# Input projection of a hybrid decoder layer: gates, keys and values 512 columns wide

## The chip, the cores and the metric

The kernel runs on one core of a Trainium2 chip. Its engines work from queues of their own, each strictly in order: TensorE (PE, matrix products into PSUM), VectorE (DVE), ScalarE (ACT), GpSimd (POOL) and SyncE (SP, which here only issues DMA transfers). They wait for each other through semaphores. The metric is the time of one execution on the device in microseconds (us); lower is better. The median of three runs of the kernel before is 3501.9 us (3501.55 to 3503.35).

## What is computed

One step of a decoder layer for one prompt of 2048 tokens and 8 sampled sequences of 8 tokens, all in float32. Cut to what matters here:

```python
z = einsum('bsd,dc->bsc', x, w_in)              # 1024 -> 3600 columns, for 2048 + 64 tokens
fq, fk, fv = z[..., 0:512], z[..., 512:1024], z[..., 1024:1536]   # attention, 8 heads of 64
flogf = log_sigmoid(z[..., 1536:1544] + b_fox_f)
qk = silu(causal_conv4(z[..., 1544:2568]))      # mLSTM queries and keys, 4 heads of 128
mv = z[..., 2568:3080]; ig, lf = gates of z[..., 3080:3088]
og = sigmoid(z[..., 3088:3600] + b_og)          # output gates
fox_h = forgetting attention (prompt: causal; samples: over 8192 cached tokens each)
m_h   = mLSTM: per head a 128 x 128 state, carried from chunk to chunk
x1 = layer_norm(a * x + concat(fox_h, norm(m_h) * og) @ w_o)
y  = layer_norm(a * x1 + square(relu(x1 @ w1)) @ w2)
```

`fk`, `fv`, the states and several small tensors are outputs too.

## The kernel before

The work runs in phases: A, the input projection (some 0 to 988 us); B, the prompt's attention; O, the output projection; C, the two matrices of the MLP. Two side streams run beside them. One is the mLSTM (`gate_stream`, `m_block`, `m_sample`), which has to end with phase A. The other is the sampled tokens' attention (`sample_attention`), which goes on to the end.

Every float32 product is made of three in the format fp32r. `split_hi` (ACT, L130) rounds an operand to its high part, `split_lo` (DVE, L133) takes the rest, and `mm3` (L138 to L140) adds hi x hi, hi x lo and lo x hi over 8 row tiles of 128. One group is thus 24 matmuls into one PSUM bank (`pm`, four banks).

Phase A goes over four blocks of tokens: the first has the 64 sampled tokens (tile 16) and four tiles of 128, the others four tiles. `load_x` transposes a tile's x on PE and splits it. Before, a block has two pairs of buffers, `xh0`/`xl0` (320 columns) and `xh1`/`xl1` (256). `wload` brings 256 (or 272) columns of `w_in` as two pieces of four row tiles: a raw slot `wra` (two of them), then a `whi` and a `wlo` slot (four of each), 4 x 272 numbers per partition. A load takes two of the four slots, and the next load can fill the other two.

A block makes, in this order: mLSTM values with the gate columns (two loads); mLSTM queries and keys, eight groups of 128 channels with a convolution behind them (four loads); output gates (two); attention queries (two); keys (two); values (two). "Natural" passes (`natural`: values, gates, keys) have tokens on the partitions: x is the stationary operand, a tile's 24 matmuls stream 256 weight columns, and a `sink` copies the bank out (`st`, four buffers of 256) and stores it. The query and key groups have channels on the partitions: weights are stationary and 320 or 256 token columns stream, two matmul groups for one block. The last tile of the values' second pass starts the next block's `load_x`.

`tick(us)` is called after each group with the time that the group is supposed to take. It emits one step of the mLSTM stream for each 2.8 us (`PACE_M`) and one step of the sampled attention for each 7.5 us. A step runs to the next `yield`. `beside` binds its instructions behind the latest ones of the main stream; beyond this, the final order in each engine's queue is set by a planner that simulates the program while it is built, and an engine then keeps that order.

The mLSTM works through 16 chunks of 128 tokens, four a block (`m_block`, L576 on). A chunk's products are the scores `pS` (L604) and transposed keys `pk` (L611) in the one `mm` bank, the numerators of two pairs of heads (L621, L622) and the state's updates (L629) in the one `mn` bank. After `norm_out` (statistics on DVE, a power and the gating on POOL) come the output transposes (L561), in the `mm` bank again, and ACT's copy of them (L563). L645 takes the last state out. In the changed kernel these lines are numbered higher by 6: L610, L617, L627, L628, L635, L567, L569, L651; the first transpose of phase B, L835, is L841.

After the last block, the steps of the mLSTM stream that are left are emitted one behind the other, and then phase B:

Of the kernel before, what the change touches and what calls it, by code (L numbers as in the profile page):

```python
# [19 lines left out]
# microseconds of the main stream's products per step of a side stream  # L20
# [24 lines left out]
C_O = 3088  # L45
# [7 lines left out]
def body(ctx, tc, I, O, stages):  # L53
# [3 lines left out]
    # ------------------------------------------------------------------ constants  # L57
# [25 lines left out]
    # pools of the sampled tokens' attention, which runs beside all phases, and of the mLSTM  # L83
# [6 lines left out]
    sqk = []                                         # new k of the sampled tokens  # L90
# [4 lines left out]
    gm = pm.tile([128, 16, 8], F32, name="gm")      # g = i - b and m, tokens on partitions  # L95
# [6 lines left out]
    def beside(gen):  # L102
        """one step of a side stream, whose instructions queue behind the main stream's latest"""
        with ExitStack() as es:
            for i in last.values():
                es.enter_context(tc.issue_after(i.ins))
            return next(gen, 0)

    def tick(us):
        """keeps the side streams in step with the main one"""  # L110
# [45 lines left out]
    # ------------------------------------------------------------------ phase A: input projection  # L156
# [16 lines left out]
    # conv weights transposed: [128 ch, 8 groups, 5] with the factor 1/2 of silu(c) = c/2 (1 + tanh(c/2))  # L173
# [38 lines left out]
    def wload(cols):  # L212
        """columns of w_in, [(first, number), ...], in their two parts, for each of the 8 row tiles"""
        n = sum(c[1] for c in cols)
        H, L = [], []
        for kg in range(2):
            wr = pa.tile([128, 4 * 272], F32, name="wra", bufs=2)[:, :4 * n].rearrange("p (k c) -> p k c", k=4)
            o = 0
            for c0, m in cols:
                SY.dma_start(wr[:, :, o:o + m], w_in[kg * 512:(kg + 1) * 512, c0:c0 + m].rearrange("(k p) c -> p k c", p=128))  # L220
                o += m
            wh = pa.tile([128, 4 * 272], F32R, name="whi", bufs=4)[:, :4 * n].rearrange("p (k c) -> p k c", k=4)
            wl = pa.tile([128, 4 * 272], F32R, name="wlo", bufs=4)[:, :4 * n].rearrange("p (k c) -> p k c", k=4)
            split_hi(wh, wr)
            split_lo(wl, wr, wh)
            H += [wh[:, k] for k in range(4)]
            L += [wl[:, k] for k in range(4)]
        return H, L
# [6 lines left out]
    xT = {}  # L235
# [10 lines left out]

    def load_x(bi, tiles):
        """the block's x with channels on partitions, in two parts; column tiles of two token tiles"""
        blk, pre, off = geom(bi)
        for t in tiles:  # L250
            i = int(off[t] >= pre + 256)
            if len(xT.setdefault(bi, [])) == i:
                w = 256 if i else 320
                xT[bi].append((pa.tile([128, 8, w], F32R, name=f"xh{i}"), pa.tile([128, 8, w], F32R, name=f"xl{i}")))
# [3 lines left out]
            (xh, xl), s = xcol(bi, t)  # L258
            for hf in range(2):
# [3 lines left out]
                dh = xh[:, hf * 4:hf * 4 + 4, s]  # L263
                split_hi(dh, px[:, :, :n])
                split_lo(xl[:, hf * 4:hf * 4 + 4, s], px[:, :, :n], dh)

    def xcol(bi, t):
        """column tile and columns of a token tile"""
        blk, pre, off = geom(bi)
        o = off[t]  # L270
        i = int(o >= pre + 256)
        o -= i * (pre + 256)
        return xT[bi][i], slice(o, o + tok_n(t))

    def gate_stream(bi):
# [4 lines left out]
        def gates(z, lg, shape, bb):  # L280
# [16 lines left out]
            # log1p(e) = ln(u) + (e - (u - 1)) / u  # L297
# [21 lines left out]
        def rowset(cols, base, n_el, np_, sample):  # L319
# [32 lines left out]
            # M = m - b (kept in lr), ar = m0 - M, g = i - b  # L352
# [28 lines left out]
            # back to tokens on partitions: g, m  # L381
# [13 lines left out]
    def block_a(bi):  # L395
# [3 lines left out]
        def natural(sink, *cols, hook=None):  # L399
            wh, wl = first.pop() if first else wload(cols)  # L400
            for i, t in enumerate(blk):
# [4 lines left out]
                (xh, xl), s = xcol(bi, t)  # L406
                for k in range(8):
                    mm3(ps, xh[:, k, s], xl[:, k, s], wh[k], wl[k], k == 0, k == 7)
                sink(t, m, ps)
                tick(2.6)  # L410

        def stage(ps, m, n):
            st = pa.tile([128, 256], F32, name="st", bufs=4)[:m, :n]
            A.copy(st, ps)
            return st
# [12 lines left out]
        # mLSTM q/k, channels on partitions, causal convolution along the free axis  # L428
        for j in range(8):
# [8 lines left out]
            for i in range(2):  # L438
                xh, xl = xT[bi][i]
                w = 256 + (pre if i == 0 else 0)  # L440
                ps = ppa.tile([128, 512], F32, name="pm", tag="pm", bufs=4)[:, :w]
                for k in range(8):
                    mm3(ps, wh[k][:, cs], wl[k][:, cs], xh[:, k, :w], xl[:, k, :w], k == 0, k == 7)
                tick(w * 0.01)
                if w == 320:
                    A.copy(qs[:, :, 3:11], ps[:, 0:64].rearrange("p (b t) -> p b t", t=8))
                A.copy(qi[:, 3 + i * 256:259 + i * 256], ps[:, w - 256:])  # L447
# [18 lines left out]
        if pre:  # L466
            # conv state of the sampled sequences
# [16 lines left out]
        for i in range(2):  # L484
            def sink(t, m, ps, i=i):
                r = tok_r(t)
                cs = slice(i * 256, (i + 1) * 256)
                st = pa.tile([128, 256], F32, name="st", bufs=4)[:m]
                V.tensor_tensor(st, ps, bog[:m, cs], op=OP.add)  # L489
                A.activation(st, st, AF.Tanh, scale=0.5)  # L490
                V.scalar_tensor_tensor(st, st, 1.0, nwh[:m, cs], op0=OP.add, op1=OP.mult)
                SY.dma_start(dog[r:r + m, cs], st)
            natural(sink, (C_O + i * 256, 256))
        gated.add(bi)
        # attention q, scaled, channels on partitions; that of the sampled tokens as [channel % 32, sequence, channel // 32, t]
        for j in range(4):
            if j % 2 == 0:
                wh, wl = wload([(j * 128, 256)])
                if pre:
                    qr = ps_.tile([32, 8, 8, 8], F32, name="qr", bufs=1)  # L500
            cs = slice((j % 2) * 128, (j % 2) * 128 + 128)
            st = pa.tile([128, 512], F32, name="qst", tag="ac", bufs=3)
            for i in range(2):
                xh, xl = xT[bi][i]
                w = 256 + (pre if i == 0 else 0)
                ps = ppa.tile([128, 512], F32, name="pm", tag="pm", bufs=4)[:, :w]
                for k in range(8):
                    mm3(ps, wh[k][:, cs], wl[k][:, cs], xh[:, k, :w], xl[:, k, :w], k == 0, k == 7)
                tick(w * 0.01)
                if w == 320:  # L510
                    for c in range(4):
                        V.tensor_scalar(qr[:, :, (j % 2) * 4 + c], ps[c * 32:c * 32 + 32, 0:64].rearrange("p (b t) -> p b t", t=8), 0.125, None, op0=OP.mult)
                A.activation(st[:, i * 256:i * 256 + 256], ps[:, w - 256:], AF.Copy, scale=0.125)
# [3 lines left out]
        for i in range(2):  # L517
            def sink(t, m, ps, i=i):
                d = k_out(t)[:, i * 256:(i + 1) * 256]
                if t == 16:  # L520
                    if i == 0:
                        sqk.append(pm.tile([64, 512], F32, name="sqk", tag="qk", bufs=1))
                    st = sqk[0][:, i * 256:(i + 1) * 256]
                    A.copy(st, ps)
                else:
                    st = stage(ps, m, 256)
                SY.dma_start(d, st)
            natural(sink, (512 + i * 256, 256))
        for i in range(2):
            def sink(t, m, ps, i=i):  # L530
                d = v_out(t)[:, i * 256:(i + 1) * 256]
                SY.dma_start(d, stage(ps, m, 256))
            natural(sink, (1024 + i * 256, 256),
# [933 lines left out]
```

## Time and profile before

| | |
|---|---|
| median of three runs | 3501.9 us |
| profiled execution: span | 3492.4 us |
| what lies around the span, against the median | 9.5 us |
| PE busy in the span | 3354.9 us, 96% |
| ACT, DVE, POOL busy | 1366.6, 2178.9, 897.4 us |
| mean granted TensorE clock | 0.985 |

The page gives no time of the profiled execution apart from its span, so the 9.5 us are against the runs' median.

How to read the rows. A page's row of groups has the line, the engine, the operation, the tile written and those read, the shapes and the count; then busy time and the mean of one in ns; then the engine's idle time just before them and what ended it. A row of the timeline has the start in us from the span's start, the length in us, the engine, the line, the operation and the count of instructions merged; in brackets the idle time ahead of it and who ended it. Matmuls are pipelined and their ends are modelled, so that neighbours overlap: what one costs in a stream is the distance of two starts. SPq is SP's queue of DMA issues. A row of windows has, for each stretch, its length, each engine's busy time and count, the TensorE clock, the DMA engines' mean busy share, and GB/s.

### The profile page before, as it was taken

Reading aid. Unit: us, or ns where it says so; the run is one execution under the profiler, and the core shown is the slowest. Engines: PE = TensorE matmul, PEld = TensorE weight load, DVE = VectorE, ACT = ScalarE, POOL = GpSimd, SP = SyncE. Lnnn points to the kernel's source line nnn. Section 1 sums busy time; section 2 is a strip of 40 time slices with the busy share of each in tenths; the row PEclk is TensorE's granted clock in tenths of the full one; section 3 lists DMA queues with packets and bytes.
Section 4 is the critical chain, followed back from the end, with each engine's and each line's share of the span. In section 5 each row is a group of like instructions: output and inputs, shape, how many; then the busy total and the mean of one; then the engine's idle time right before and its main releaser. Section 6 shows DMA issues by size and latency. Waiting matters only on the chain.

```text
span 3492.4 us, 59522 instructions
## 1 busy us (share of the span) xinstructions
PE 3354.9 (96%) x22428; PEld 2670.1 (76%) x22428; DVE 2178.9 (62%) x5302; ACT 1366.6 (39%) x2818; POOL 897.4 (26%) x942
## 2 busy tenths in 40 slices
PE   8899899999989999999899999999999999999998
PEld 8898778888866666667567677677677777898887
DVE  6747747657558787655556567666666544654555
ACT  3333323334358888512324243332233333443332
POOL 1013213231322222265332324223324111100000
PEclk9999999999999999999899999999999999999999
DMA  6557777775853232586776767768768555442221
GB/s 198 167 167 223 223 220 237 245 246 174 275 163 86 75 81 57 172 275 215 273 250 197 266 214 262 258 200 271 253 218 296 192 164 176 148 154 73 85 85 64
DMA packets 446040, 663.15 MB, mean 190 GB/s; under 512 B 84604, under 2 KB 333760, under 8 KB 444856
## 3 DMA queue, kind: packets, MB, share of 16 engines
q1 hardware_dynamic: 369064, 380.13, 36.1%
q0 software_dynamic: 74304, 270.57, 22.5%
q10 hardware_dynamic: 2384, 8.65, 0.7%
q8 instruction: 176, 2.88, 0.3%
q14 instruction: 112, 0.92, 0.1%
HBM read 598.01 MB, written 61.22 MB: 189 GB/s over the span
## 4 chain that ended last, share of the span: by engine, by line
PE 69%; DMA 15%; DVE 6%; issue 5%; POOL 3%; ACT 1%; SPq 0%; POOLq 0%; DVEq 0%; ACTq 0%
PE py L138 7%; PE py L140 6%; PE py L139 6%; PE ph L138 6%; PE ph L139 6%; PE ph L140 6%; DMA kraw<-cache_k,idxK 4%; PE po L919 4%; DMA vt<-cache_v,idxV 4%; PE pt L910 4%; PE pm L138 4%; PE pm L139 3%; PE pm L140 3%; PE sO L1406 3%; PE pS L871 2%
## 5 line engine op out<-in xcount | busy, mean ns | idle before, releaser
L1150 DVE TENSOR_TENSOR y<-y,py 128x512 f32<-128x512 f32 (+1 forms) x476 | 319.3, 680 | 251.1 <-PE py L140 246.9
L138 PE MATMUL ph<-x1h,wh 128*128 128x512 f32 (+1 forms) x1280 | 455.5, 356 | 2.4 <-ACT wh L130 2.4
L130 ACT ACTIVATE wh<-wr 128x1024 fp32r<-128x1024 f32 x264 | 273.4, 1057 | 466.0 <-PE py L140 264.0
L139 PE MATMUL ph<-x1l,wh 128*128 128x512 f32 (+1 forms) x1280 | 454.7, 355 | 0.0
L140 PE MATMUL ph<-x1h,wl 128*128 128x512 f32 (+1 forms) x1280 | 453.7, 355 | 0.2 <-DVE wl L133 0.2
L1401 POOL DMA_INDIRECT vt<-cache_v,idxV x256 | 257.9, 1007 | 736.1 <-PE sO L1406 701.2
L1316 DVE STREAM_TRANSPOSE kT<-kraw 128x512 f32<-128x512 f32 x512 | 328.3, 684 | 179.8 <-DMA kraw<-cache_k,idxK 178.4
L138 PE MATMUL py<-wh,hh 128*128 128x512 f32 (+1 forms) x1088 | 431.6, 399 | 1.5 <-DVE y L1148 0.8
L139 PE MATMUL py<-wl,hh 128*128 128x512 f32 (+1 forms) x1088 | 429.6, 395 | 0.7 <-DVE wl L133 0.7
L140 PE MATMUL py<-wh,hl 128*128 128x512 f32 (+1 forms) x1088 | 429.1, 395 | 0.0
L1314 POOL DMA_INDIRECT kraw<-cache_k,idxK x256 | 280.9, 1097 | 571.3 <-DVE kT L1316 439.0
L133 DVE TENSOR_TENSOR wl<-wr,wh 128x1024 fp32r<-128x1024 f32 x264 | 333.2, 1269 | 91.4 <-PE ph L140 25.7
L138 PE MATMUL pm<-whi,xh 128*128 128x256 f32 (+2 forms) x1088 | 320.3, 294 | 7.5 <-DVE st L489 4.8
L139 PE MATMUL pm<-wlo,xh 128*128 128x256 f32 (+2 forms) x1088 | 315.7, 290 | 0.0
L140 PE MATMUL pm<-whi,xl 128*128 128x256 f32 (+2 forms) x1088 | 315.4, 290 | 0.0
L138 PEld LDWEIGHTS ph<-x1h,wh 128*128 128x128 f32 x1280 | 240.9, 188 | 46.5 <-issue 11.1
L140 PEld LDWEIGHTS ph<-x1h,wl 128*128 128x128 f32 x1280 | 240.7, 188 | 42.8 <-issue 11.1
L139 PEld LDWEIGHTS ph<-x1l,wh 128*128 128x128 f32 x1280 | 240.6, 188 | 40.4 <-issue 8.6
L138 PEld LDWEIGHTS py<-wh,hh 128*128 128x128 f32 (+1 forms) x1088 | 201.3, 185 | 62.7 <-issue 18.1
L140 PEld LDWEIGHTS py<-wh,hl 128*128 128x128 f32 (+1 forms) x1088 | 201.3, 185 | 55.5 <-issue 9.9
L139 PEld LDWEIGHTS py<-wl,hh 128*128 128x128 f32 (+1 forms) x1088 | 201.5, 185 | 48.5 <-issue 8.6
L138 PE MATMUL pm<-xh,whi 128*128 128x256 f32 (+1 forms) x768 | 224.7, 293 | 0.8 <-ACT qi L447 0.8
(359 smaller groups left out, 6875.1 us busy)
## 6 DMA issues: line engine op xcount, KB each, us to landing
wr<-w SPq DMA_DIRECT2D x256, 512.0 KB
wra<-w_in SPq DMA_DIRECT2D x112, 512.0 KB
xn<-x_prompt SPq DMA_DIRECT2D x32, 512.0 KB
Rb<-dR SPq DMA_DIRECT2D x128, 128.0 KB
dqk<-th SPq DMA_DIRECT2D x32, 256.0 KB
qk<-dqk SPq DMA_DIRECT2D x16, 512.0 KB
qn<-dq SPq DMA_DIRECT2D x128, 64.0 KB
wr<-w_o SPq DMA_DIRECT2D x16, 512.0 KB
```

The source lines that it names most:

```text
L130: last["ACT"] = A.activation(dst, src, AF.Copy, scale=scale)
L133: r = (eng or V).tensor_tensor(dst, src, hi.bitcast(F32), op=OP.subtract)
L138: T.matmul(ps, wh, xh, start=first, stop=False)
L139: T.matmul(ps, wh, xl, start=False, stop=False)
L140: last["PE"] = T.matmul(ps, wl, xh, start=False, stop=stop)
L910: T.transpose(pt[:, k], sc[i][0][k0 // 4][:, k * 128:(k + 1) * 128], ident)
L919: last["PE"] = T.matmul(po[c:c + 64, q0:], z["vn"][:, k], PT[:, k - k0, q0:], start=(k < 2), stop=(k >= nk - 2), skip_group_check=True)
L1150: V.tensor_tensor(y, y, ps, op=OP.add)
L1314: G.indirect_dma_start(out=kraw, out_offset=None, in_=ck, in_offset=IO(ap=idxK[:, b, kt + k, f:f + 1], axis=0))
L1316: V.transpose(z["kT"][:, k, 2 * f + i].rearrange("p b c -> p (b c)"), kraw[:, i * 512:(i + 1) * 512])
L1401: G.indirect_dma_start(out=vt.rearrange("p f c -> p (f c)"), out_offset=None, in_=cv, in_offset=IO(ap=idxV[:, b, pg * 4 + u, f:f + 1], axi ...
L1406: T.matmul(po[r:r + 32], z["PT"][:, hg, 2 * f + g, pg].rearrange("p h q -> p (h q)"), vt[:, g, hg * 256:(hg + 1) * 256], start=(kt == 0 an ...
```

## The change

Output gates, attention keys and attention values are projected in one pass of 512 columns each. Their load comes as four pieces of two row tiles, into the same slots; one load fills all four. A block's x lies in one pair of buffers (`xh`, `xl`, made once), in block 0 as 320 and 256 columns for each row tile, in the later blocks tile after tile, so that a group with channels on the partitions streams 512 columns as four runs of 128. `st` has three buffers of 512, a wide natural group ticks 5.2 once, and `qr` takes the slot of `Rb`. mLSTM values with the gate columns, and the weight loads of queries and keys, stay at 256 or 272 columns.

```diff
 def wload(cols):
-        for kg in range(2):
-            wr = pa.tile([128, 4 * 272], F32, name="wra", bufs=2)[:, :4 * n]...
+        q = 4 if n <= 272 else 2
+        for kg in range(8 // q):
+            wr = pa.tile([128, 4 * 272], F32, name="wra", bufs=2)[:, :q * n]...
...
+    xh = pa.tile([128, 36 * 128], F32R, name="xh")
+    xl = pa.tile([128, 36 * 128], F32R, name="xl")
...
+    def xpiece(bi):
+        if bi == 0:
+            return [(320, *(x[:, :2560].rearrange("p (k c) -> p k c", k=8) for x in (xh, xl))),
+                    (256, *(x[:, 2560:].rearrange("p (k c) -> p k c", k=8) for x in (xh, xl)))]
+        return [(512, *(x[:, :4096].rearrange("p (t k c) -> p k t c", t=4, k=8) for x in (xh, xl)))]
...
 def natural(sink, *cols, hook=None):
-                    mm3(ps, xh[:, k, s], xl[:, k, s], wh[k], wl[k], k == 0, k == 7)
+                    mm3(ps, th[:, k], tl[:, k], wh[k], wl[k], k == 0, k == 7)
                 sink(t, m, ps)
-                tick(2.6)
+                tick(2.6 if wh[0].shape[1] < 512 else 5.2)
 def stage(ps, m, n):
-            st = pa.tile([128, 256], F32, name="st", bufs=4)[:m, :n]
+            st = pa.tile([128, 512], F32, name="st", bufs=3)[:m, :n]
...
-            for i in range(2):
-                xh, xl = xT[bi][i]
-                w = 256 + (pre if i == 0 else 0)
+            for w, th, tl in xpiece(bi):
                 ps = ppa.tile([128, 512], F32, name="pm", tag="pm", bufs=4)[:, :w]
                 for k in range(8):
-                    mm3(ps, wh[k][:, cs], wl[k][:, cs], xh[:, k, :w], xl[:, k, :w], k == 0, k == 7)
+                    mm3(ps, wh[k][:, cs], wl[k][:, cs], th[:, k], tl[:, k], k == 0, k == 7)
                 tick(w * 0.01)
...
-            natural(sink, (C_O + i * 256, 256))
+        natural(sink, (C_O, 512))
...
-                    qr = ps_.tile([32, 8, 8, 8], F32, name="qr", bufs=1)
+                    qr = ps_.tile([32, 8, 8, 8], F32, name="qr", tag="Rb", bufs=1)
...
-            natural(sink, (512 + i * 256, 256))
+        natural(sink, (512, 512))
...
-            natural(sink, (1024 + i * 256, 256),
-                    hook=None if i == 0 or bi == 3 else lambda n: load_x(bi + 1, BLKS[bi + 1][0:1]) if n == len(blk) - 1 else None)
+        natural(sink, (1024, 512),
+                hook=None if bi == 3 else lambda n: load_x(bi + 1, BLKS[bi + 1][0:1]) if n == len(blk) - 1 else None)
```

105 lines of the change are left out of this document (50 added, 55 removed).

## The prediction

> **What bounds the kernel now.** I read the page first (engines, chain), then three windows, then the end of the projection in order of time.
>
> ```profile
> span 3492.4 us, 59522 instructions
> PE 3354.9 (96%) x22428; PEld 2670.1 (76%) x22428; DVE 2178.9 (62%) x5302; ACT 1366.6 (39%) x2818; POOL 897.4 (26%) x942
> PE 69%; DMA 15%; DVE 6%; issue 5%; POOL 3%; ACT 1%; SPq 0%; POOLq 0%; DVEq 0%; ACTq 0%
> L138 PE MATMUL pm<-whi,xh 128*128 128x256 f32 (+2 forms) x1088 | 320.3, 294 | 7.5 <-DVE st L489 4.8
> ```
> ```profile
> core 0: us, PE busy (x) PEld busy (x) DVE busy (x) ACT busy (x) POOL busy (x), PEclk, DMA share, GB/s
> 0.00:988.00 988.00, 920.77 (x7692) 843.84 (x7693) 621.60 (x1725) 330.25 (x714) 236.50 (x251) 0.98 0.70 214
> 988.00:1001.40 13.40, 4.72 (x30) 3.56 (x29) 6.21 (x27) 3.34 (x9) 5.24 (x9) 0.83 0.74 196
> 1001.40:3492.40 2491.00, 2429.39 (x14711) 1822.67 (x14709) 1551.07 (x3550) 1032.97 (x2095) 655.67 (x682) 0.99 0.56 180
> ```
> PE is busy 96% of the span and carries 69% of the chain. The projection (0 to 988) keeps PE at 921 of 988 us, so a shorter stream of products shortens it. The 13.4 us behind it are another regime: PE works 4.72 us of them and waits otherwise. There the mLSTM's last chunk finishes with no products beside it, and prompt attention begins only behind it:
>
> ```profile
> 987.64 0.28 PE L140 MATMUL pm<-whi,xl 128*128 128x256 f32 x1
> 987.76 0.38 PE L621 MATMUL mn<-va,Wm 128*128 128x129 f32 x2
> 990.20 0.49 PE L621 MATMUL mn<-va,Wm 128*128 128x129 f32 x2 [1.38 <-ACT hh L573]
> 992.72 0.71 PE L629 MATMUL mn<-va,kw 128*128 128x129 f32 x4 [1.36 <-ACT hh L573]
> 999.35 1.12 PE L561 MATMUL mm<-ident,hh 128*128 128x128 f32 x4 [4.51 <-POOL hh L557]
> 1001.19 0.38 PE L645 MATMUL mm<-ident,Cs 128*4 128x128 f32 x1 [0.72 <-ACT ot L563]
> 1001.36 1.91 PE L835 MATMUL pt<-ident,dup 128*128 128x128 f32 x8
> ```
> The last product starts at 987.64, the attention's first transpose at 1001.36: an open tail of 13.7 us.
>
> **The change, part by part.** The sum is made against the profiled execution: span 3492.4, which lies 9.5 us under the 3501.9 median of the runs; I take those 9.5 as unchanged and add the difference to the median.
>
> *Wider products.* Natural groups of output gates, k and v: 17 token tiles x 3 kinds x 24 matmuls = 1224 of 512 columns in place of 2448 of 256. Channel groups: 12 x 24 x 3 blocks = 864 in place of 1728 (block 0 keeps 320 + 256). What one costs on the path is start to start, not its busy time:
>
> ```profile
> 304.88 0.28 PE L140 MATMUL pm<-xh,wlo 128*128 128x256 f32 x1
> ...
> 309.31 0.28 PE L138 MATMUL pm<-xh,whi 128*128 128x256 f32 x1
> ```
> ```profile
> 1899.63 0.39 PE L139 MATMUL ph<-x1l,wh 128*128 128x512 f32 x1
> ...
> 1900.77 0.39 PE L138 MATMUL ph<-x1h,wh 128*128 128x512 f32 x1
> ```
> 37 steps between the first two: 4.43 / 37 = 0.1197 us. 5 between the others: 1.14 / 5 = 0.228. A pair saves 0.239 - 0.228 = 0.0114 us; x 2088 = **-24 us**. In blocks 1 to 3 the streamed operand becomes four pieces of 128 columns, 4 KB apart, which no fp32r row here shows: the upper end is 0.239 for these 864 (nothing saved, -14 in all). The lower end is the rounding of the rows, 0.01 us over 5 steps: 0.226, -28. I take 0.228, as each piece is contiguous.
>
> The Trainium skill (TensorE: Matmul & The Clock Gate, section Back-to-back issue gap) puts a lone warm matmul at N / 2.4 + 2.5 ns, so a pair would save 2.5 ns, an estimate of -5 us where the rows give -24, and the total 19 us later. The trace disagrees: its 256-column pitch lies 13 ns over 256 / 2.4, not 2.5.
>
> *Weights.* Four pieces of two row tiles fill all four `whi`/`wlo` slots, so a 512-wide load cannot lie ready beside another, and only two raw pieces (`wra`, two slots) wait ahead.
>
> ```profile
> 404.01 0.38 SPq L220 DMA_DIRECT2D wra<-w_in  x1
> ...
> 944.42 0.37 SPq L220 DMA_DIRECT2D wra<-w_in  x1
> ```
> ```profile
> 408.85 1.06 ACT L130 ACTIVATE whi<-wra 128x1024 fp32r<-128x1024 f32 x1 [2.23 <-DMA wra<-w_in]
> ...
> 957.00 1.06 ACT L130 ACTIVATE whi<-wra 128x1024 fp32r<-128x1024 f32 x1
> ```
> ```profile
> L130 ACT ACTIVATE whi<-wra x112: 1039/1058/1121, 6.1 to 957.0; 128x1024 fp32r<-128x1024 f32 x104, 128x1088 fp32r<-128x1088 f32 x8
> L133 DVE TENSOR_TENSOR wlo<-wra,whi x112: 1179/1224/2351, 7.2 to 958.1; 128x1024 fp32r<-128x1024 f32 x104, 128x1088 fp32r<-128x1088 f32 x8
> ```
> From k to v, clock from the start of k's last tile (24 x 0.228 = 5.5 us): the first slot is free after 6 matmuls, 1.4; + 1.06 + 1.22 = 3.7, when the raw slot is free and the third raw piece can be issued on SP's queue; landed and waited for 4.84 later, 8.5; split 9.6. In the changed kernel's PE order, block 1 has 20 products and 4 transposes of v ahead of the first that needs that piece: 5.5 + 20 x 0.228 = 10.0. So the row with nothing else in the way just fits. The split queues behind other ACT and DVE work and the load behind others on SP: lower end 0, upper end 8 us a block (the projection's last load is split 12.6 after its issue, 944.42 to 957.00, its wait for a slot included; 12.6 - 4.84). I take 2 us x 4 for v, 1 us in all for q behind the gates: **+9**, range 0 to 31. The other passes find two slots freed a pass earlier.
>
> The Trainium skill (Trainium Kernel Development and Optimization, section Best Practices) says to double-buffer so that DMA and compute overlap; before did it, this gives it up for 512-wide loads. No row prices it at a boundary here.
>
> *One x buffer, three `st` of 512, `qr` on `Rb`'s slot.* A token tile's columns are overwritten only after its own v products, three tiles earlier than the rewrite, so nothing. Half as many evictions, twice as wide, lie beside PE (PE's idle before `pm<-whi,xh` products is 7.5 us in the page's row). The stores keep their bytes. `qr` is done before the first `Rb` load. Zero; the cover is the product stream, and without it each eviction would show with its copy:
>
> ```profile
> 984.70 0.37 ACT L414 COPY st<-pm 128x256 f32<-128x256 f32 x1 [4.15 <-PE pm L140]
> ```
>
> *Side streams.* `tick(5.2)` once for two `tick(2.6)`: as many steps, two at a time. Here the PE order of the changed kernel speaks. Numbers behind names count tiles as they are made:
>
> ```
> before 6197 L611 mm_11792 (pk, last chunk)  next to pm_11764, pm_11803
> before 6222 L140 pm_11803  = last product;  6223 L621 ... 6237 L645, 6238 L835 attention
> after  4046 L617 mm_8473   (pk, chunk 12)   inside pm_9317; made before pm_8498 (row 3662)
> after  4092 L140 pm_9381   = last product;  4093 L635, 4097 L567 (chunk 12)
> after  4100 L610, 4118 L610, 4136 L610 (chunks 13, 14, 15)  ... 4154 L651, 4155 L841 attention
> ```
> Before, the mLSTM stands level with the products at the end; after, it runs most of a block's second half behind, and **three whole chunks** queue in order between the last product and the attention, with nothing among them. Price of an uncovered chunk:
>
> ```profile
> 162.34 1.16 PE L604 MATMUL mm<-qk 128*128 128x128 f32 x8 [2.80 <-DMA qk<-dqk]
> 166.59 0.60 PE L611 MATMUL mm<-ident,qk 128*128 128x128 f32 x4
> 167.03 0.39 PE L621 MATMUL mn<-va,Wm 128*128 128x129 f32 x2
> 167.25 0.39 PE L622 MATMUL mn<-Cs,qa 128*128 128x129 f32 x2
> ```
> ```profile
> 1000.55 0.58 ACT L563 COPY ot<-mm 128x512 f32<-128x512 f32 x1 [1.50 <-PE mm L561]
> ```
> First product with keys to first numerator, 4.7 (162.34 to 167.03); numerator to output transposes, 11.6 (987.76 to 999.35); these to the end of their copy, which frees the one `mm` bank for the next chunk, 1.8 (999.35 to 1001.13). Sum 18.1. Chunk 12's second numerators end some 14 products (3.2 us) before the last product; their transposes come 9.15 later (990.20 to 999.35), copied at +7.7. Then 3 x 18.1 and the state's end, 0.2: attention at **+62 us** instead of 13.7, so **+48**. Lower end: 13.7 a chunk, as the whole tail of before, +35. Upper: the shortest distance of two chunks that the paced stream shows,
>
> ```profile
> 664.86 1.16 PE L604 MATMUL mm<-qk 128*128 128x128 f32 x8 [0.69 <-ACT ot L563]
> 690.74 1.05 PE L604 MATMUL mm<-qk 128*128 128x128 f32 x8
> ```
> 25.9, +72. I take 18.1, because the tail's rows are unpaced like those to come. In turn this PE work leaves the product stream: chunks 13, 14 and parts of 12 and 15, 15 us of busy by the rows above, of which start to start (0.22 for 0.39 shown at 167.03) about 11 are real: **-11**.
>
> *Sum:* -24 + 9 + 48 - 11 = +22. Span 3514, median **3524**. Ends: -28 + 0 + 35 - 11 = -4 and -14 + 31 + 72 - 11 = +78.
>
> **Rivals.**
> 1. *The tail stays hidden: faster.* If the three chunks run into each other (the next chunk's loads and exponentials done while the last normalises, the `mm` bank never the limit), the tail falls. It decides at 11 us a chunk: 3 x 7.1 less is the whole +22. At 7 us (PE work and waits for the state alone) the tail adds 15: -24 + 9 + 15 - 11 = -11, 3491. For it: PE works only 4.72 of 13.4 us. Against it: one `mm` bank, and transposes standing ahead of the next chunk's first product in PE order. Chance 0.10.
> 2. *Weights arrive late at every wide pass.* 31 in place of 9: 3546. For it: DMA is 0.70 busy in the projection. Against it: PE order sets three tiles' products on the first pieces. Chance 0.13.
> 3. *A 512-wide matmul saves nothing* (two pitches of 256): -24 goes, 3548. The skill's gap rule above leads near it, 3543. For it only the strided operand; the 0.228 row speaks against. Chance 0.05.
> 4. *Gains and tail cancel*, chunk at 13.7 and no late weights: -24 + 35 - 11 = 0, 3502. Chance 0.12.
>
> **How the numbers follow.** The forecast has 0.60; its own range is 3509 to 3540. 0.2% (7 us) is about what a measurement tells here. Faster is case 1, 0.10; same is case 4, 0.12; slower is the rest, 0.78. The range 3495 to 3552 leaves out most of case 1 and the far ends of 2 and 3.
>
> **What would show it.** Right: in the profile after, products of 512 at 0.228 start to start; the last product near 960 (988 - 24 - 11 + 9 = 962); then some 60 us with PE mostly idle, waits on `hh` of POOL and ACT, three `pS` about 18 apart, attention near 1024; everything later as long as before (2491). Wrong: attention starting within 30 us of the last product, PE waits on `whi` of more than 5 us at v, or a later stage that changes length, since the order there is planned anew too.

## The result, and the profile after

The kernel after takes 3511.6 us (median of 20 runs, 3502.4 to 3525.2) against 3500.5 us for the kernel before (20 runs beside them, 3490.9 to 3516.9). The ratio is 1.0037, 95% interval 1.0025 to 1.0049: about 13 us slower (9 to 17). 3524 was forecast, +22 us, with 3509 to 3540 as the range of that case. The direction and the mechanism came out as forecast; the sum was some 10 us too high, chiefly because the part behind the attention's start, put at no change, got 11 us shorter. Within the tail, two of the three chunks cost more than the 18.1 us taken for each.

First the head of the page of the kernel after, with its row for the channel groups:

```profile
span 3505.9 us, 55033 instructions
PE 3350.7 (96%) x20340; PEld 2561.7 (73%) x20340; DVE 2174.7 (62%) x5268; ACT 1359.6 (39%) x2731; POOL 906.1 (26%) x942
PE 53%; DMA 9%; issue 4%; DVE 2%; POOL 2%; ACT 1%; POOLq 0%; ACTq 0%; SPq 0%; DVEq 0%
L138 PE MATMUL pm<-whi,xh 128*128 128x512 f32 (+5 forms) x680 | 245.8, 364 | 3.2 <-ACT whi L130 3.0
```

2088 matmuls are gone (22428 to 20340) and PE is still 96% busy: this average cannot show a loss of 13 us. The stretches can. The same three as in the prediction: the product stream, the open tail behind it, and the rest from the attention's first transpose on (length, busy time and instructions of each engine, granted clock, DMA share, GB/s):

```profile
0.00:959.60 959.60, 895.33 (x5498) 714.62 (x5499) 600.08 (x1620) 310.48 (x600) 229.12 (x235) 0.97 0.69 216
959.60:1026.00 66.40, 34.23 (x134) 27.80 (x133) 23.79 (x98) 13.21 (x36) 16.96 (x26) 0.54 0.53 141
1026.00:3505.90 2479.90, 2421.19 (x14711) 1819.29 (x14710) 1550.80 (x3550) 1035.94 (x2095) 660.00 (x682) 0.99 0.55 180
```

The stream is 28.4 us shorter (988 to 959.6), the tail 53 us longer (13.4 to 66.4), the rest 11.1 us shorter (2491.0 to 2479.9). The sum, +13.5, is the difference of the two spans. The middle row is the loss: PE issues 134 matmuls where before it issued 30, is busy 34 of the 66 us, and its mean granted clock is 0.54.

PE's order of events in that tail (start, duration, line, operation; in brackets the idle time ahead and what ended it), cut to the last product, the first product with keys of each chunk (`L610`), one chunk's numerators and output transposes, and the attention's first transposes:

```profile
959.31 0.39 PE L140 MATMUL pm<-whi,xl 128*128 128x512 f32 x1
...
965.59 1.12 PE L567 MATMUL mm<-ident,hh 128*128 128x128 f32 x4 [3.70 <-POOL hh L563]
967.38 2.08 PE L610 MATMUL mm<-qk 128*128 128x128 f32 x8 [0.68 <-ACT ot L569]
...
971.98 0.64 PE L627 MATMUL mn<-va,Wm 128*128 128x129 f32 x2
...
976.14 0.80 PE L627 MATMUL mn<-va,Wm 128*128 128x129 f32 x2 [2.23 <-ACT hh L579]
...
980.80 1.23 PE L635 MATMUL mn<-va,kw 128*128 128x129 f32 x4 [2.57 <-ACT hh L579]
...
985.19 1.12 PE L567 MATMUL mm<-ident,hh 128*128 128x128 f32 x4 [1.24 <-POOL hh L563]
988.50 2.08 PE L610 MATMUL mm<-qk 128*128 128x128 f32 x8 [2.19 <-ACT ot L569]
...
1008.89 2.07 PE L610 MATMUL mm<-qk 128*128 128x128 f32 x8 [0.72 <-ACT ot L569]
...
1026.03 1.91 PE L841 MATMUL pt<-ident,dup 128*128 128x128 f32 x8
```

Three whole chunks stand here one behind the other, as the changed PE order said. From first key product to first key product they lie 21.1 and 20.4 us apart, the third needs 17.1 to the attention's start, and nothing else stands among them in PE's order. Each chunk waits for the copy that frees the one `mm` bank (`ot`), for its normaliser (`hh` on ACT, then POOL), and inside its numerators for the one `mn` bank (the 2.23 and 2.57 on `hh L579`; 1.39 and 1.36 in the next chunk).

### The profile page after: what moved, and what is told of

It reads as the page before. It is cut to its first block, busy times and chain, and to the rows that moved or that the text cites. A ratio compares the mean times of both kernels' runs of the same rounds, so it can differ in the third digit from the quotient of the medians.

```text
span 3505.9 us, 55033 instructions
## 1 busy us (share of the span) xinstructions
PE 3350.7 (96%) x20340; PEld 2561.7 (73%) x20340; DVE 2174.7 (62%) x5268; ACT 1359.6 (39%) x2731; POOL 906.1 (26%) x942
## 4 chain that ended last, share of the span: by engine, by line
PE 53%; DMA 9%; issue 4%; DVE 2%; POOL 2%; ACT 1%; POOLq 0%; ACTq 0%; SPq 0%; DVEq 0%
PE py L138 6%; PE py L140 6%; PE py L139 6%; PE ph L138 5%; PE ph L139 5%; PE ph L140 5%; PE po L925 4%; DMA vt<-cache_v,idxV 4%; PE pt L916 4%; DMA kraw<-cache_k,idxK 3%; PE sO L1412 2%; PE pS L877 2%; PE pS L878 2%; PE sQ L1333 1%; DMA wr<-w 1%
## 5 line engine op out<-in xcount | busy, mean ns | idle before, releaser
L138 PEld LDWEIGHTS ph<-x1h,wh 128*128 128x128 f32 x1280 | 241.1, 188 | 46.1 <-issue 11.1
L140 PEld LDWEIGHTS ph<-x1h,wl 128*128 128x128 f32 x1280 | 240.8, 188 | 44.2 <-issue 11.1
L138 PE MATMUL pm<-whi,xh 128*128 128x512 f32 (+5 forms) x680 | 245.8, 364 | 3.2 <-ACT whi L130 3.0
L139 PE MATMUL pm<-wlo,xh 128*128 128x512 f32 (+5 forms) x680 | 244.6, 361 | 0.6 <-DVE wlo L133 0.6
L140 PE MATMUL pm<-whi,xl 128*128 128x512 f32 (+5 forms) x680 | 244.0, 359 | 0.0
L1412 PE MATMUL sO<-vt,PTs 128*32 128x256 f32 x2048 | 190.0, 395 | 34.2 <-DMA vt<-cache_v,idxV 33.5
```

What stands on the lines that cost most here:

```text
L138: T.matmul(ps, wh, xh, start=first, stop=False)
L139: T.matmul(ps, wh, xl, start=False, stop=False)
L140: last["PE"] = T.matmul(ps, wl, xh, start=False, stop=stop)
L1412: T.matmul(po[r:r + 32], z["PT"][:, hg, 2 * f + g, pg].rearrange("p h q -> p (h q)"), vt[:, g, hg * 256:(hg + 1) * 256], start=(kt == 0 an ...
```

## The experiments

In one session the runs share the runs of the kernel before. Its median was 3484 to 3500 us in the four sessions, so only ratios within one are compared. For each profile I give the last product, the tail (last product to the attention's first transpose) and that transpose's start; the kernel before has 987.6, 13.7 and 1001.4.

### Each half of the change alone

The shared x buffer stays; in the first kernel the natural passes go back to two of 256 (and `st` to its four buffers of 256), in the second the channel groups of blocks 1 to 3 do:

```diff
-        natural(sink, (512, 512))                    # e1: keys; gates and values alike
+        for i in range(2):
+            natural(sink, (512 + i * 256, 256))
-        return [(512, *(x[:, :4096].rearrange("p (t k c) -> p k t c", t=4, k=8) for x in (xh, xl)))]   # e2
+        return [(256, *(x[:, i * 2048:i * 2048 + 2048].rearrange("p (t k c) -> p k t c", t=2, k=8)
+                        for x in (xh, xl))) for i in range(2)]
```

> The kernel after with only the channel groups of blocks 1 to 3 at 512 columns; output gates, keys and values back to two passes of 256. In its PE order one whole mLSTM chunk stands behind the last product (three in the kernel after, none in the kernel before). Theory T (the time is the shorter products plus the chunks that they leave uncovered): 864 pairs x (0.2394 - 0.226) = -12 us of products; the tail is 66.7 - 2 x 20.4 = 26 us instead of 13.7, +12; PE work of that chunk out of the stream, -4. Attention starts 4 us earlier than before, the total is -4 (from -15 to +2), no wait of PE on whi. Rival S (the loss comes from somewhere that each part of the change brings by itself, such as the shared x buffer): +5 us, as 864 of 2088 pairs of the +12 measured for the whole.

> The kernel after with only the output gates, keys and values at 512 columns; the channel groups of blocks 1 to 3 back to two matmul groups of 256. In its PE order one whole mLSTM chunk stands behind the last product. Theory T: 1224 pairs x 0.0134 = -16 us of products; waits for weights +6 as in the kernel after (PE on whi and wlo); tail 26 instead of 13.7, +12; -4 of PE work moved. Total -2 us (from -14 to +4). Rival S: +7 us, as 1224 of 2088 pairs of the +12. If the two halves together come to less than -3 while the whole is +12, the loss is the two chunks more that only the whole leaves uncovered (T); if they add up to about +12, it is S.

Channels alone: 3477.3 us, ratio 0.9982 (0.9971 to 0.9993), last product 970.4, tail 27.6, attention 998.0. Natural alone: 3487.8 us, ratio 1.0008 (0.9996 to 1.0021), last product 979.0, tail 29.6, attention 1008.6. One chunk behind the products makes 28 to 30 us of tail, three make 67. Together the halves come to about -3.5 us (-6.3 and +2.8 by the ratios, each within some 4 us), the whole to +13: the loss is not in either half but in what only the whole leaves uncovered, and S falls. T held, though the natural half's +2.8 is near the end of its range. The natural half's last product is 5 us later than T's terms give (987.6 - 16 + 6 - 4 = 974); I come back to that.

### The chunks' price without any wide product

In the kernel before, the mLSTM's steps of the last block are given out so late that three chunks stand behind the last product:

```diff
+    pace = [PACE_M]
-        while macc[1] and macc[0] > PACE_M:
+        while macc[1] and macc[0] > pace[0]:
...
+        if bi == 3:
+            pace[0] = 14.0
```

> The kernel before with one number changed: in the last block a step of the mLSTM is given out every 14.0 us of products instead of 2.8, so that three whole chunks stand behind the last product, as in the kernel after, with products still 256 wide. Measures the tail's price by itself. Theory T: last product 11 us earlier than before (near 977), tail 67 us instead of 13.7, attention at 1043, +42. If the 11 us that the kernel after won back behind the attention's start come from the longer tail (loads for later stages done in it, a clock that recovers), they come back here too: total +31. If they belong to the change or to chance, the total is +42. Rival C (tail cheap, the lost time lies elsewhere): under +15.

3510.2 us, ratio 1.0068 (1.0053 to 1.0083), +24 us. PE's events, again only the last groups ahead of the tail, the key products and the attention's start:

```profile
974.62 0.60 PE L630 MATMUL mn<-va,kw 128*128 128x129 f32 x4
...
976.48 1.05 PE L605 MATMUL mm<-qk 128*128 128x128 f32 x8
...
995.58 2.08 PE L605 MATMUL mm<-qk 128*128 128x128 f32 x8 [0.73 <-ACT ot L564]
...
1016.24 2.08 PE L605 MATMUL mm<-qk 128*128 128x128 f32 x8 [0.72 <-ACT ot L564]
...
1033.37 0.84 PE L838 MATMUL pt<-ident,dup 128*128 128x128 f32 x3
```

Chunks 19.1 and 20.7 us apart with 256-wide products too. Last product 974.5, 13 us earlier than before (the prediction's "moved out" term, 11; 10.5 earlier than in the second profile of before, below); tail 58.9, +45 (the prediction's tail term, 48); attention +32. T had a tail of 67 and +42: here the first key products start 2 us behind the last product, 8 in the kernel after. So uncovered chunks cost nearly what the prediction took, with products of either width. C (tail cheap) falls. The total is 8 us under the +32 at the attention, so T's second half, too, had to be looked at: see the repeats below.

### A second bank for the numerators

```diff
-  tag="pm", bufs=4      (PSUM banks of the products)
+  tag="pm", bufs=3
-  name="mn", bufs=1     (PSUM banks of the mLSTM's numerators and state updates)
+  name="mn", bufs=2
```

> The kernel after with one PSUM bank moved from the products (pm: 4 to 3) to the mLSTM's numerators (mn: 1 to 2); nothing else. In its PE order no chunk starts behind the last product. Theory T: the tail returns to 15 us or less; the last product comes 11 us later than in the kernel after (the chunks' PE work is back among the products), near 970; attention near 984, 17 us ahead of the kernel before; PE waits a little more for evictions with three banks, 0 to 6. Total -17 us against before (from -25 to -8), that is 25 to 30 us under the kernel after: faster than both. Rival B (three banks stall the products): last product at 985 or later and PE waits on st and qst evictions of over 15 us; total about as before. Rival L (the tail's length isn't made by the chunks): attention stays over 30 us behind the last product.

3469.4 us, ratio **0.9964** (0.9948 to 0.9980): 12.5 us faster than the kernel before and, by the two ratios, about 25 us faster than the kernel after; it is the only one of the kernels with wide natural passes that beats before. Its PE events from the last product on:

```profile
973.33 0.39 PE L140 MATMUL pm<-whi,xl 128*128 128x512 f32 x1
973.57 0.60 PE L617 MATMUL mm<-ident,qk 128*128 128x128 f32 x4
974.00 0.39 PE L627 MATMUL mn<-va,Wm 128*128 128x129 f32 x2
...
974.89 0.39 PE L627 MATMUL mn<-va,Wm 128*128 128x129 f32 x2
...
976.58 0.71 PE L635 MATMUL mn<-va,kw 128*128 128x129 f32 x4 [0.63 <-ACT hh L579]
...
983.40 1.12 PE L567 MATMUL mm<-ident,hh 128*128 128x128 f32 x4 [5.22 <-POOL hh L563]
986.88 0.38 PE L651 MATMUL mm<-ident,Cs 128*4 128x128 f32 x1 [2.37 <-ACT ot L569]
987.05 1.27 PE L841 MATMUL pt<-ident,dup 128*128 128x128 f32 x5
```

The second pair of numerators (974.89) follows the first without a wait, where in the kernel after it waited 2.23 us for `hh`, and the state update waits 0.63 instead of 2.57. With this shorter chain no whole chunk is left: last product 973.3 (expected 970), tail 13.7, attention 987.1 (expected 984). The Trainium skill (Perfetto Trace Analysis, section Matmuls under Optimizing Tensor Performance) says that independent matmul groups should rotate through different PSUM banks, so that one's evacuation overlaps the next group; this run agrees for the numerators, with the 2.23 us gone.

Two controls for this: the bank moved in the kernel before, and in the kernel after the product bank taken away but not given to the numerators.

```diff
-  tag="pm", bufs=4 ;  name="mn", bufs=1      (kernel before)
+  tag="pm", bufs=3 ;  name="mn", bufs=2
-  tag="pm", bufs=4                           (kernel after)
+  tag="pm", bufs=3
```

> The kernel before with one PSUM bank moved from the products (4 to 3) to the mLSTM's numerators (1 to 2), products 256 wide as before. Theory T (the second bank pays only where whole chunks would be left over, and before leaves none): last product and tail as before within 5 us, total 0 (from -5 to +6). Rival G (the second bank is worth some 15 us in any kernel, and has nothing to do with the wide products): -10 or lower.

> The kernel after with three PSUM banks for the products in place of four and the fourth left unused; numerators keep one bank. In its PE order two whole chunks stand behind the last product. Theory T (the numerators' single bank makes the chain of a chunk long, and this the lag): tail 43 to 55 us, last product 959 to 968, total +5 (from 0 to +12). Rival P (fewer banks for the products pull the mLSTM forward, the second bank for numerators does nothing): tail under 20 us, total -15 as with the bank moved.

Before with the bank moved: 3519.9 us, ratio 1.0085 (1.0065 to 1.0105), +30 us; last product 1010.4, tail 12.9. So the bank is no general gain (G falls), but T's "0" was wrong as well: with this change the stream is 23 us longer. After with three product banks: 3503.1 us, ratio 1.0029 (1.0013 to 1.0044), +10; last product 992.1, tail 36.8. Two whole chunks still stand in the tail, so fewer product banks alone don't pull the chunks in (P falls); but one of the three did go back among the products, the tail is shorter than T's 43 to 55, and the stream is 24 us longer than T's 968. Both kernels have a stream some 25 us longer with three banks; the one with wide products and two numerator banks does not. In neither is there one wait of PE that explains it. In the kernel before with the bank moved, against the second profile of before, 13 of the 25 us are idle time of PE (77.8 against 64.7), in many small waits, and 12 are busy time of the same 7691 matmuls; the clock's record (last section) shows 65 us at half in this stream against 41, which would be worth 12. Why two numerator banks make up for it only beside wide products, no run shows.

### Giving the steps out otherwise

```diff
-                tick(2.6 if wh[0].shape[1] < 512 else 5.2)
+                    if k == 3 and wh[0].shape[1] == 512:    # e10, within the group of 8 row tiles
+                        tick(2.6)
+                tick(2.6)                                   # and the channel groups alike
-PACE_M = 2.8
+PACE_M = 2.0      # e11;  e9: 2.4, with the second numerator bank
```

> The kernel after, with the side streams' steps given out in two halves within each 512-wide group (after four of its eight row tiles, and at its end) instead of two at once at the end. In its PE order three whole chunks still stand behind the last product. Theory T (the lag is the length of the mLSTM's own chain against a shorter product stream): tail 62 to 69 us, +13 as the kernel after (from +8 to +18). Rival H (steps in pairs make the lag): tail under 30 us, total -15 or lower.

> The kernel after with the mLSTM's steps given out every 2.0 us of products in place of 2.8 and four banks for the products. In its PE order two whole chunks stand behind the last product. Theory T: the tail falls by one chunk, 20 us, to 46; the last product 4 us later; total -3 us against before (from -8 to +4). Rival E (giving out steps late is the cause): tail under 20 us, total -15 or lower.

> The kernel with the bank moved to the numerators, and the mLSTM's steps given out every 2.4 us of products instead of 2.8. In its PE order 5 groups of mLSTM matmuls stand behind the last product in place of 17. Theory T (the open tail is what is left to win): tail 5 to 10 us instead of 13.7, total -19 us against before (from -27 to -10). Rival N (the steps given out earlier stand in front of products and wait there): tail shorter, but the last product later by as much; total -14 as without it.

Halved ticks: 3511.8 us, ratio 1.0086 (1.0071 to 1.0101), tail 76.4. That is +30. H falls: two steps at a time are not what puts the mLSTM behind (T's own number, +13, was too low by 17; below). Steps given out every 2.0: 3485.5 us, ratio 1.0007 (0.9997 to 1.0017), tail 37.3, but last product 982.8, 23 us later than in the kernel after in place of 4. E falls: the total is better than that of the kernel after and no better than before, as more of the waits now lie among the products (PE is idle 75 us of their stream, against 64 and 67 in the kernel after). With two numerator banks and 2.4: tail 6.2, last product 1001.3, ratio 1.0017 (1.0004 to 1.0029); T forecast -19, N -14, it was +6. In this profile PE waits 19.1 us for `xn` ahead of the next block's transposes:

```profile
PE px L280 <- DMA xn<-x_prompt: 19.1, 4, 8.2
```

where the kernel after waits 10.3 (waits table below). At neither of the two paces tried does giving the steps out earlier beat the kernel before; the second bank at the old pace does.

### The rest of the change, and the two kernels again

The kernel after with every group at 256 columns (and `st` in four buffers of 256) keeps only the shared x buffer, the load's code and the slot of `qr`:

```diff
-        natural(sink, (C_O, 512))                    # keys and values alike
+        for i in range(2):
+            natural(sink, (C_O + i * 256, 256))
-        return [(512, *(x[:, :4096].rearrange("p (t k c) -> p k t c", t=4, k=8) for x in (xh, xl)))]
+        return [(256, *(x[:, i * 2048:i * 2048 + 2048].rearrange("p (t k c) -> p k t c", t=2, k=8)
+                        for x in (xh, xl))) for i in range(2)]
```

> The kernel after with every group of products back at 256 columns: what is left of the change is the x columns of a block in one buffer, the piecewise weight load's code (four row tiles a piece, as before) and the new slot of the sampled queries. In its PE order nothing stands behind the last product that does not in the kernel before. Theory T (these parts cost nothing): last product 984 to 990, tail 13 to 15, total 0 (from -7 to +5). Rival X (the shared buffer holds back the next block's transposes): waits before px on PE above the 10 us of before by 5 us or more, total +5 or higher. If the part behind the attention's start is 2472 to 2485, it is shorter for any new order of the program; if 2488 to 2497, the wide products made it shorter.

> The kernel before, unchanged, for a second profile. From the attention's first transpose to the end its first profile shows 2491.1 us; the kernel after 2479.8, and the four kernels run since 2473.1 to 2483.5. Theory V (the 11 us that the kernel after won back behind the attention's start are the scatter from one execution to the next): this profile shows 2472 to 2485. Theory W (they belong to the change): 2488 to 2494 again. In both, last product 985 to 990 and a tail of 13 to 15 us.

> The kernel after, unchanged, beside the others on the same chip. Last product 956 to 963, tail 64 to 69 us, attention to end 2472 to 2485 under V and 2478 to 2482 under W. Total +13 us against before (from +8 to +18).

Buffers only: 3484.4 us, ratio 0.9998 (0.9982 to 1.0015), last product 985.4, tail 14.2. These parts cost nothing that can be told from zero (-6 to +5 us). X falls: the waits ahead of `px` on `xn` are 6.8 + 4.6 us, before 5.4 + 4.7. Before again: one time of 3496.7, last product 985.0, tail 13.8. After again: 3505.3 us, ratio 1.0042 (1.0023 to 1.0062), last product 959.7, tail 66.8.

For the 11 us behind the attention's start, V falls: before again shows 2496.1 us from there to the end, after again 2477.0. W's ranges were missed too, by 2 and by 1 us, on the side that makes the difference larger. I split that part in all profiles at the first product of the last stage (`ph`):

```
us, by kernel                attention's start  last stage
                             to last stage      to the end
before / again                  700.5 / 704.9     1790.6 / 1791.2
after / again                   690.2 / 691.8     1789.6 / 1785.2
channels only, natural only     691.8, 697.5      1781.3, 1780.0
second mn bank                  694.7             1783.8
before, late chunks             698.3             1785.2
before with second mn bank      697.7             1785.1
three pm banks                  692.2             1787.3
fine ticks                      703.8             1772.8
pace 2.0 / mn bank, pace 2.4    689.3 / 698.6     1778.8 / 1784.1
buffers only                    701.1             1780.0
```

The last stage, whose code is the same in all, scatters from 1773 to 1791, and roughly with the session (1790 where before had 3500 us, 1785 to 1791 where it had 3493, 1773 to 1785 where it had 3484). The middle part scatters less: two profiles of one kernel agree within 4.4 us (before) and 1.6 (after), and the kernel after is 10 to 13 us shorter there than before, in both pairs. Its gain is real. Buffers only shows 2481 us from the attention's start to the end, which its expectation would have read as "shorter for any new order"; the split says otherwise: its middle part is as long as that of before, and its last stage is short like the others of its session.

In the middle part PE issues the same matmuls in all four profiles of before and after (4397 or 4398 by the windows). It is busy 674 and 675 us of it before, 667.5 and 667.4 after, and idle 26 and 30 us before, 23 and 24 after. So 7 or 8 of the 10 to 13 us are the same matmuls in less time. The clock's record shows 38 and 39 us at half there before, 28 and 30 after; half of that difference, some 5 us, would be the most that it explains.

The gain does not come from the wide products as such (after with halved ticks has them and 703.8) nor from the long tail (the same kernel has the longest). Of the three kernels without wide products two are 2 to 7 us shorter than before, and the third is as before. What is left is the order that comes out when the program is planned anew; no run shows that by itself. One wait can be seen. Eleven us behind the attention's first transpose the kernel before has a wait (2.1 us in its second profile) that the kernel after has not:

```profile
1012.50 0.44 PE L871 MATMUL pS<-ks,qh 128*128 128x384 f32 x1 [1.47 <-DVE mx L878]
```

And the gap between the last product of the output projection and the first of the last stage is 30.3 and 30.4 us before, 25.7 and 25.7 after. PE is idle 12 us of it in both, mostly for the sampled attention's gathered values; what differs is work (18 us against 14), as less of that side stream lies there. Which instruction's place decides was not tried and stays open. The halved ticks fit: their attention starts 5 us later than in the kernel after, and their middle part is 14 us longer.

## Why the prediction was right or wrong

*Wider products, -24: right.* In the kernel after the strided channel products start

```profile
956.81 0.39 PE L138 MATMUL pm<-whi,xh 128*128 128x512 f32 x1
...
959.08 0.39 PE L139 MATMUL pm<-wlo,xh 128*128 128x512 f32 x1
```

10 steps in 2.27 us, 0.227 each. Streaming four pieces 4 KB apart costs nothing against the 0.228 of the last stage; rival 3 is out. So is the -5 that the prediction worked out by the gap rule of the Trainium skill (TensorE: Matmul & The Clock Gate, section Back-to-back issue gap): the pitches here, 0.1197 and 0.227, give 12 ns a pair and -26.

*Weights, +9: the waits are 6, but only half of what happens there.* PE's waits on weights in the product stream are 6.1 us, in six waits (5.5 in the second profile). From the list of its waits there (engine, tile and line, what it waited for: us in all, times, longest):

```profile
PE px L280 <- DMA xn<-x_prompt: 10.3, 5, 3.0
PE px L483 <- DVE scT L475: 5.8, 1, 5.8
PE sO L1412 <- DMA vt<-cache_v,idxV: 5.6, 3, 4.0
...
PE pm L138 <- ACT whi L130: 3.0, 3, 1.3
PE pm L140 <- DVE wlo L133: 2.5, 1, 2.5
...
PE pm L139 <- DVE wlo L133: 0.6, 2, 0.4
```

Rival 2 (31) is out. But the prediction set the evictions at zero. In the same stretch of the kernel before, products waited for evictions and x:

```profile
PE pm L138 <- DVE st L489: 4.8, 1, 4.8
...
PE pm L138 <- ACT qi L447: 2.1, 2, 1.3
...
PE pm L138 <- DVE xl L133: 1.1, 1, 1.1
```

These 8 us are gone in the kernel after (0.2 left; in the second pair of profiles 7.4 against 4.7). They were not won: PE waits longer elsewhere, for `xn` (10.3 and 7.9 us in the two profiles of after, 5.4 and 3.9 before) and for `scT` (5.8 and 4.5 against 0.4). PE's idle time in the product stream is 67.2 and 64.7 us in the profiles of before (988.0 - 920.8 in the first) and 64.3 and 67.3 in those of after (959.6 - 895.3 in the first): the same within what two profiles of one kernel differ by. An engine that stands still for other reasons as long as before gains nothing from a shorter wait at one place.

*Moved out of the stream, -11: right; the last product at 962:* 959.3 and 959.7. In the kernel with late chunks PE's busy time in the stream is 11.0 us less than before (909.8 against 920.8). -26 by the pitch and -11 make -37 of busy time; measured are -25.5 and, in the second pair, -27.9. So some 9 to 11 us of gain are missing. PE's idle time, where the prediction put its +9 for weights, did not grow; that the +9 nearly hit the place of the last product is luck. The natural half alone misses 5 as well. Part of it is clock: the trace's record of the granted clock shows 37 and 41 us at half in the product streams of the two profiles of before, 61 and 48 in those of after. Half of the difference is work not done, if PE was busy all that time: an estimate of 12 us at most in the first pair and 3 in the second. The rest is open.

*The tail, +48: right in kind, 5 us low.* +53 in the kernel after, +45 with narrow products. The three chunks take 21.1, 20.4 and 17.1 us, for 18.1 each; 8.1 us lie ahead of them, for 7.7. The three pieces of that price in the second chunk of the tail, whose key products stand at 988.50 and whose successor's at 1008.89 above:

```profile
992.37 0.64 PE L627 MATMUL mn<-va,Wm 128*128 128x129 f32 x2
...
1007.06 1.12 PE L567 MATMUL mm<-ident,hh 128*128 128x128 f32 x4 [4.76 <-POOL hh L563]
```

3.9 for 4.7 (key products to first numerator), 14.7 for 11.6 (numerator to output transposes), 1.8 for 1.8 (these to the next chunk). The last chunk needs 11.3 for the middle piece (1012.77 to 1024.02). The prediction took its 11.6 from the tail of before, which is also a last chunk. What a last chunk lacks is a successor: in the second one, POOL's gating of `hh` (L563) stands behind the next chunk's preparation (L602, L603, L605, L612), which waits for the load of `Wm`; from the normalised `hh` of DVE (L561) to its start 3.7 us pass, in the last chunk 0.2:

```profile
1000.97 1.12 DVE L561 TENSOR_SCALAR hh<-hh,mv,r 128x128 f32<-128x128 f32 x4
...
1002.39 1.28 ACT L602 ACTIVATE Wm<-Wm,gm 128x128 f32<-128x128 f32 x4 [3.29 <-DMA Wm<-dM]
...
1003.79 0.64 POOL L603 TENSOR_SCALAR_AFFINE_SELECT Wm<-Wm 128x512 f32<-128x512 f32 x1 [2.86 <-ACT Wm L602]
1004.39 1.26 POOL L605 TENSOR_TENSOR qa<-qa,qk 128x512 f32<-128x512 f32 x1
1005.60 0.19 POOL L612 COPY wkc<-Wm 128x4 f32<-128x4 f32 x1
1005.74 1.26 POOL L563 TENSOR_TENSOR hh<-hh,og 128x512 f32<-128x512 f32 x1
...
1021.36 1.12 DVE L561 TENSOR_SCALAR hh<-hh,mv,r 128x128 f32<-128x128 f32 x4
...
1022.70 1.27 POOL L563 TENSOR_TENSOR hh<-hh,og 128x512 f32<-128x512 f32 x1 [1.38 <-PE mn L635]
```

So chunks did run into each other, as rival 1 supposed, but to the cost of the one that was finishing. The kernel with late chunks has 14.8 and 15.0 for this piece where a chunk follows, 11.3 at the end. In the kernel with three product banks POOL makes the gating ahead of the successor's steps (L563 at 1008.72, L603 at 1009.95), and that chunk takes 17.2 us from key products to key products. Not in the price either was the clock (last section). Attention started at 1026.0; 1024 was predicted: some 3 us too late for the last product and 5 too short for the tail nearly cancel, which is luck. Rivals 1 and 4 needed a chunk at 11 or 13.7.

*"Everything later as long as before (2491)": this step failed.* It is 2479.8, then 2477.0 against 2496.1. The prediction named it under what would make it wrong, "since the order there is planned anew too", but gave it no term and no bounds. In the spans: -28 (forecast -26) and +53 (+48) and -11 (0) make +13.5 in place of +22. What made that part shorter is shown in part only (busy time and clock above).

## What to carry to other kernels

A stream that runs beside the main one has a length of its own; when the main stream gets shorter, count what of the other no longer fits beside it, chunk by chunk, and price it at its chain, not at its engine time. Take that price from a chunk that another one follows. Here a matmul pair 12 ns cheaper lost to three chunks of 17 to 21 us, and one PSUM bank moved to the side chain, whose waits on the bank it took away, turned +13 us into -12; giving the side work out earlier at two other paces did not. And whatever is planned as a whole moves everywhere when one part changes: give the untouched stages a term with bounds instead of zero (here the middle part moved by 10 to 13 us).

## What the runs showed of the hardware

PE's clock fell to half in the open tail although PE was busy 34 of its 66 us. In the kernel after the eight key products take 2.08 us in place of the 1.05 that the kernel with late chunks shows 2 us behind its last product, 7.5 us before its clock falls, and the attention begins at half rate too:

```profile
1030.17 0.63 PE L877 MATMUL pS<-ks,qh 128*128 128x512 f32 x1
1030.59 0.63 PE L878 MATMUL pS<-ks,ql 128*128 128x512 f32 x1
...
1033.48 0.48 PE L877 MATMUL pS<-ks,qh 128*128 128x512 f32 x1
1033.79 0.39 PE L878 MATMUL pS<-ks,ql 128*128 128x512 f32 x1
```

0.42 us apart and 0.63 long at first; 0.39 long, as in the full stream, 3 us later. Full rate is 0.227 apart. The trace's record of the granted clock shows 68 us at half around the tail of after, 10 and 17 around those of before. The Trainium skill (TensorE: Matmul & The Clock Gate, section Wait — 56ns, not 53.3ns?) gives 426.7 ns as the cold start-to-start of 512 columns; the rows agree with 0.42. Bursts of products between waits of 1 to 5 us were not enough here to bring the full clock back for 60 us, and a chunk cost about 1.5 us more: in the kernel with late chunks the first one, whose key products and numerators still ran at full clock, takes 19.1 us to the next key products, and the second, all at half, 20.7.
